# Retention by tiles with a carried state, and row transposes in two halves, in a one-core decoder layer

## The chip, the core and the metric

The kernel runs on one core of a Trainium2 chip. The metric is the device time of one execution in microseconds. A core has TensorE (matmuls; PE in the profile, its weight loads PEld), VectorE (DVE), ScalarE (ACT), GpSimd (POOL) and SyncE (SP), which here only issues DMAs. Each engine takes its own instructions in order and waits on semaphores for the others. TensorE writes to PSUM, eight banks of 128 partitions by 512 fp32 values.

## What is computed

The reference is one decoder layer on 512 tokens of width 1024. Cut to what the change touches:

```python
def _retention(q, k, v):            # 8 heads of 64, chunks of c = 128
    log_g = log(1 - 2 ** (-5 - arange(h)))
    dmat = where(diff >= 0, exp(log_g * diff), 0)
    scores = einsum('bhnid,bhnjd->bhnij', qc, kc) * dmat
    inner = einsum('bhnij,bhnjd->bhnid', scores, vc)
    kv = einsum('bhnjd,bhnje->bhnde', kc * k_dec, vc)
    # state' = g_chunk * state + kv; cross = (qc @ state) * q_dec
    return inner + cross

def _moe(xt, ...):                  # 32 experts, top 4
    hgu = xb @ w_up_gate[e] + b_up_gate[e]
    hact = x_glu * sigmoid(1.702 * x_glu) * (x_lin + 1)
    return hact @ w_down[e] + b_down[e]
```

Ahead of these stand a norm, one input projection and stick-breaking attention, whose result is yA; the retention's result, normed by groups and gated, is yB. Both go through one output projection with a residual. Behind the experts come a gate and a small projection of a per-layer input.

## The kernel before

The kernel is written in a tile framework. Outside of blocks with an order by hand, a planner puts each engine's instructions in order at build time, by the order in the program, by readiness and by its own cost estimates. On the chip that order is fixed.

**Projections and attention.** `proj` multiplies x by slices of the input weights, split into a high and a low part (`split`, L158, L159), three matmuls for each product. `ret_qk` (L326) takes the retention's q and k: `evacuate` gives four row tiles `ns` of 128 tokens, each normed and rotated on VectorE (L338 to L341); q is multiplied by its norm (L343), and k's norm is kept in `rkr` for later. `to_T` transposes them into `rqT` and `rkT`, with two heads side by side on the 128 partitions. `val` makes `vR`, whose mean over each head is taken off at L580 to L582.

**Retention, L593 to L632.** A loop over four pairs of heads (`hp`). For each tile `b` of 128 keys, the scores of that tile against all queries from it on (L607: 512, 384, 256 and 128 columns) go to PSUM banks 0 to 3 in rotation (`zbank`); VectorE scales them by the key's norm and by a decay table made by ScalarE (L613 and L599; the table has a zero above the diagonal through `dif`, L422 to L426), and L618 multiplies them by `vR` into `py`, bank 4 or 5. The two heads of a pair use two halves of the TensorE array. Behind the tiles stands a chain: copy and square on ScalarE, a mean over the head by a matmul (L625), Ln and Exp, two VectorE operations, and the split into the two parts of yB (L631, L632).

**Output projection.** `wo_half` (L635) adds for one row tile and half of the columns twelve 512-column matmuls in bank 6 or 7 and one VectorE add into `acc`. The yA half of it stands behind the retention in the program, without an order by hand: 96 matmuls. The yB half, the router and what follows are in an order by hand from L862 on. The tiles of the early pools are freed behind the retention; SyncE's next loads (L672 on) wait for that.

**Expert loop.** The 32 experts' weights, 12 MB each, pass through a ring of nine slots of 2 MB; six pieces an expert, four for `up` and two for `down`. SyncE issues the next piece into a slot when TensorE has read the old one (`load_behind`). For each expert: `up` (L1103), `act_in` and `act_out` on VectorE and ScalarE (L1139 to L1147), `up32` (L1117) if more than 64 rows were routed to it, `turn_in` for the next expert's rows, `h_T` (L1153) and `down` (L1161) in three steps, `dispatch`, which gathers the rows of the expert after the next, and `down32` (L1174). `turn_in` transposes the 96 gathered rows of the next expert, eight transposes in two banks and two ScalarE copies (`turn`, L914 to L920). `turn`, `h_T`, `spread` and `down32` take their banks from `dbank`, which alternates between 2 and 3.

Of the kernel before, what the change touches and what calls it, by code (L numbers as in the profile page):

```python
# [8 lines left out]
F32 = mybir.dt.float32  # L9
# [4 lines left out]
AF = mybir.ActivationFunctionType  # L14
ALU = mybir.AluOpType
# [4 lines left out]
P = 128  # L20
S = 512
NT = S // P
D = 1024
KD = D // P
HD = 64
NH = 8
NP = NH // 2
E = 32
# [11 lines left out]
C = 96  # L40
# [10 lines left out]
def layer_kernel(ctx, tc, a, out, dbg=None, stop=None):  # L51
    nc = tc.nc
# [48 lines left out]
    def bank(i, name):  # L101
        return ps.tile([P, 512], F32, name=name, tag=f"b{i}")
# [223 lines left out]
    def ret_qk(w, name, key, tag, ahead=0):  # L326
        ns = evacuate(proj(w, name, ahead), name)
        dst = early.tile([P, NP, S], F32, name=name + "T", tag=tag)
        rst = early.tile([P, NT, NH], F32, name=name + "r")
        for t in range(NT):  # L330
            n = ns[t]
            r, _ = headnorm_rstd(n, f"{name}{t}", rst[:, t, :])
            m = e2.tile([P, 512], F32, name=f"m{name}{t}", tag="tmp")
            nv, mv = heads(n), heads(m)
            for h in range(2):
                o = slice(h * 32, h * 32 + 32)
                s2 = slice(32 - h * 32, 64 - h * 32)
                nc.vector.tensor_tensor(mv[:, :, o], nv[:, :, s2],  # L338
                                        stab[key][:, t, None, o].to_broadcast([P, NH, 32]), op=ALU.mult)
            nc.vector.tensor_tensor(nv, nv, ctab[key][:, t, None, :].to_broadcast([P, NH, HD]), op=ALU.mult)  # L340
            nc.vector.tensor_tensor(n, n, m, op=ALU.add)  # L341
            if key == "q":
                nc.vector.tensor_tensor(nv, nv, r[:, :, None].to_broadcast([P, NH, HD]), op=ALU.mult)  # L343
            to_T(n, dst, t, None, f"{name}{t}")
        return dst, rst

    def val(w, name, ahead=0):
        banks = proj(w, name, ahead)
# [70 lines left out]
    nc.gpsimd.memset(gmean, 0.0)  # L419
    for h in range(2):  # L420
        nc.gpsimd.memset(gmean[h * HD:(h + 1) * HD, h * HD:(h + 1) * HD], 1.0 / HD)
    dif = early.tile([P, S], F32, name="dif")  # L422
    nc.gpsimd.iota(dif, pattern=[[1, S]], base=0, channel_multiplier=-1, allow_small_or_imprecise_dtypes=True)
    msk = e2.tile([P, S], F32, name="msk", tag="tmp")
    nc.vector.tensor_scalar(msk, dif, 0.0, 1.0e6, op0=ALU.is_lt, op1=ALU.mult)
    nc.vector.tensor_tensor(dif, dif, msk, op=ALU.add)  # L426


    yA, yB = [mid.tile([P, 2, NP, S], F32R, name=f"y{i}", tag=f"y{i}") for i in "AB"]
# [2 lines left out]
    def zbank(name, ids):  # L432
        zn[0] += 1
        return bank(ids[zn[0] % len(ids)], name)
# [117 lines left out]
            last_silu = nc.scalar.activation(gD[:, c, :], gD[:, c, :], AF.Silu)  # L552
    with tc.issue_after(last_silu.ins):
        nc.scalar.preload_act_table_set("natural_log_exp_and_others")
    rkT, rkr = ret_qk(w_rk, "rk", "k", "kT", 200)
    wo, woh, wol = [], [], []

    def by_rows(t):
# [31 lines left out]
    wo_split(1, fresh(1, "woh1", F32R), fresh(2, "wol1", F32R))  # L590
    load(0)

    for hp in range(NP):  # L593
        hss = [slice(j * HD, (j + 1) * HD) for j in range(2)]
        decs = []
        for j in range(2):
            h = 2 * hp + j
            dec = e2.tile([P, S], F32, name=f"dec{h}", tag="tmp")
            nc.scalar.activation(dec, dif, AF.Exp, scale=math.log(1.0 - 2.0 ** (-5.0 - h)))  # L599
            decs.append(dec)  # L600
        py = bank(4 + hp % 2, f"ry{hp}")
        for b in range(NT):
            N = S - b * P
            zs, scs = [], []
            for j in range(2):
                z = zbank(f"rz{hp}{j}{b}", (0, 1, 2, 3))
                nc.tensor.matmul(z[:, :N], rkT[hss[j], hp, b * P:(b + 1) * P], rqT[hss[j], hp, b * P:S],  # L607
                                 start=True, stop=True)
                zs.append(z)
            for j in range(2):  # L610
                h = 2 * hp + j
                sc = e2.tile([P, N], F32, name=f"rs{h}{b}", tag=f"wt{b}")
                nc.vector.scalar_tensor_tensor(sc, zs[j][:, :N], rkr[:, b, h:h + 1], decs[j][:, :N],  # L613
                                               op0=ALU.mult, op1=ALU.mult)
                scs.append(sc)
            for j in range(2):
                h = 2 * hp + j
                nc.tensor.matmul(py[hss[j], b * P:S], vR[:, b, h * HD:(h + 1) * HD], scs[j],  # L618
                                 start=b == 0, stop=b == NT - 1)
        yc = e2.tile([P, S], F32, name=f"yc{hp}", tag="tmpn", bufs=4)  # L620
        nc.scalar.copy(yc, py)
        sq = e2.tile([P, S], F32, name=f"rsq{hp}", tag="tmpn", bufs=4)
        nc.scalar.activation(sq, yc, AF.Square)
        var = zbank(f"var{hp}", (0, 1, 2, 3))
        nc.tensor.matmul(var, gmean, sq, start=True, stop=True)  # L625
        nc.scalar.activation(sq, var, AF.Ln, bias=eps)
        nc.scalar.activation(sq, sq, AF.Exp, scale=-0.5)
        nc.vector.scalar_tensor_tensor(yc, yc, pcol[:, GN_G + hp:GN_G + hp + 1], sq, op0=ALU.mult, op1=ALU.mult)
        nc.vector.scalar_tensor_tensor(yc, yc, pcol[:, GN_B + hp:GN_B + hp + 1], gD[:, hp, :],
                                       op0=ALU.add, op1=ALU.mult)  # L630
        nc.scalar.activation(yB[:, 0, hp, :], yc, AF.Copy)  # L631
        nc.vector.tensor_tensor(yB[:, 1, hp, :], yc, f32(yB[:, 0, hp, :]), op=ALU.subtract)  # L632
# [253 lines left out]

    def dbank(name):
        dn[0] += 1
        return bank(2 + dn[0] % 2, name)

    def spread(e, name):
        rk = dbank("rk" + name)
# [18 lines left out]
        xgs[e] = xg_tile(f"{e}")  # L911
        return gather(rk, C, slot, xgs[e], f"{e}")

    def turn(xg, n, xT, name):  # L914
        for h in range(2):
            pt = dbank(f"px{name}{h}")
            pv = pt[:, 0:4 * n].rearrange("p (k s) -> p k s", s=n)
            for k in range(4):
                nc.tensor.transpose(pv[:, k, :], xg[0:n, (4 * h + k) * P:(4 * h + k + 1) * P], ident[0:n, 0:n])  # L919
            nc.scalar.copy(xT[:, 4 * h:4 * h + 4, 0:n], pv)  # L920
# [157 lines left out]

    xTs = {}

    def turn_in(e):
        xTs[e] = ringC.tile([P, KD, C], F32, name=f"xT{e}", tag="xT")
        turn(xgs[e], C, xTs[e], f"{e}")

    def two(j):
        return slice(j * 64, (j + 1) * 64)
# [198 lines left out]
    for e in range(E):  # L1285
# [211 lines left out]
```

## Time and profile before

| what | us |
|---|---|
| median of 3 runs (1484.51 to 1488.26) | 1484.77 |
| the profiled execution | 1485.39 |
| its span, first to last instruction | 1483.5 |
| TensorE busy in it | 1353.6 (91%) |
| VectorE, ScalarE, GpSimd busy | 451.4, 293.3, 182.4 |

Durations come from the profiled execution. The mean granted TensorE clock is 0.985 of full speed. A record of a matmul overlaps the next one's, since matmuls are pipelined: the time that one takes in a stream is read from start to start. fp32 matmuls appear as two instructions each, so that a pair of heads makes four. A DMA share is the busy share of the core's 16 DMA engines; records that touch make it go to 1.01 or 1.02. An idle time in brackets names what the engine waited for; PEq and DVEq are the engine's own instruction stream.

### The profile page before, as it was taken

What the parts mean: (1) busy time and instruction counts of PE and PEld (TensorE: products, weight loads), DVE (VectorE), ACT (ScalarE), POOL (GpSimd) and SP (SyncE); (2) the same over time, 40 slices, a digit from 0 to 9 for tenths busy, and PEclk for the clock granted to TensorE, in tenths of its full rate; (3) what the DMA queues carried; (4) which work ended last, traced back from release to release, by engine and by line L of the source; (5) the groups of instructions that cost most, each with busy time, mean ns of one, the idle gap of its engine ahead of it and who ended that gap; (6) DMA issues with size and microseconds to landing.
All of it is one profiled execution on the core that took longest, in us unless ns stands there. A gap on an engine that the chain in (4) does not pass through costs nothing. (4 is left out here: it accounts for less than half of the span.)

```text
span 1483.5 us, 21634 instructions
## 1 busy us (share of the span) xinstructions
PE 1353.6 (91%) x8629; PEld 652.0 (44%) x8629; DVE 451.4 (30%) x1033; ACT 293.3 (20%) x564; POOL 182.4 (12%) x268
## 2 busy tenths in 40 slices
PE   8999999997999999999988899878999889799788
PEld 6776775463333334334333333323333333233256
DVE  4657497545111111111211111111111121032353
ACT  5645674341010000000000001000000000111133
POOL 3132000011110111010101011000111100212230
PEclk9999999998999999999999999999999999999999
DMA  7202504167999999999999999999999999989931
GB/s 286 85 29 79 143 25 170 38 250 278 362 375 410 408 390 403 413 411 414 412 392 411 410 408 412 411 397 417 408 410 394 374 413 408 398 346 403 420 131 57
DMA packets 65528, 474.81 MB, mean 320 GB/s; under 512 B 9485, under 2 KB 10033, under 8 KB 32401
## 3 DMA queue, kind: packets, MB, share of 16 engines
q1 hardware_dynamic: 54192, 441.69, 74.7%
q0 software_dynamic: 11200, 31.22, 6.0%
q8 instruction: 97, 1.59, 0.4%
q14 instruction: 39, 0.31, 0.1%
HBM read 454.40 MB, written 18.48 MB: 319 GB/s over the span
## 5 line engine op out<-in xcount | busy, mean ns | idle before, releaser
L1161 PE MATMUL yb<-ring,hT 128*64 128x512 f32 x1024 | 245.6, 612 | 35.3 <-DVE hT L1154 27.4
L1103 PE MATMUL glu<-ring,xT 128*64 128x512 f32 x1024 | 247.6, 599 | 16.3 <-DMA ring<-in_w_up_gate_dram 16.3
L1103 PE MATMUL lin<-ring,xT 128*64 128x512 f32 x1024 | 245.5, 594 | 0.0
L1139 DVE TENSOR_SCALAR gl<-glu 128x512 f32<-128x512 f32 x32 | 22.1, 692 | 530.7 <-PE glu L1103 530.7
L1103 PEld LDWEIGHTS glu<-ring,xT 128*64 128x64 f32 x1024 | 81.9, 138 | 145.5 <-issue 115.8
L1103 PEld LDWEIGHTS lin<-ring,xT 128*64 128x64 f32 x1024 | 83.0, 137 | 139.5 <-issue 139.5
L1161 PEld LDWEIGHTS yb<-ring,hT 128*64 128x64 f32 x1024 | 65.7, 137 | 152.8 <-issue 100.8
L903 POOL DMA_INDIRECT xg<-hn_d,idx x32 | 30.5, 954 | 781.3 <-DVE idx L902 469.0
L1117 PE MATMUL u<-ring,xT 128*32 128x256 f32 x2048 | 113.3, 379 | 0.0
L1140 ACT ACTIVATE sg<-gl 128x512 f32<-128x512 f32 x32 | 20.1, 629 | 408.8 <-DVE gl L1139 408.8
L1117 PEld LDWEIGHTS u<-ring,xT 128*32 128x32 f32 x2048 | 61.6, 110 | 47.4
L1174 PE MATMUL yc<-ring,hv 128*32 128x256 f32 x1024 | 58.6, 381 | 8.3 <-DVE hv L1170 8.3
L1185 ACT COPY y<-yb 128x512 f32<-128x512 f32 x31 | 18.1, 585 | 231.9 <-PE yb L1161 222.1
L920 ACT COPY xT<-px 128x384 f32<-128x384 f32 x64 | 27.7, 482 | 155.5 <-PE px L919 155.4
L1174 PEld LDWEIGHTS yc<-ring,hv 128*32 128x32 f32 x1024 | 31.6, 110 | 31.3 <-DVE hv L1170 12.1
L919 PE MATMUL px<-ident,xg 96*128 96x96 f32 x256 | 28.9, 258 | 15.4 <-PEq L1314 8.1
L1187 POOL DMA_DIRECT2D y_d<-y x62 | 33.7, 548 | 68.7 <-ACTq L1334 39.1
L919 PEld LDWEIGHTS px<-ident,xg 96*128 96x128 f32 x256 | 23.2, 145 | 34.9 <-issue 24.2
L1181 POOL DMA_DIRECT2D y_d<-yv x64 | 31.6, 501 | 54.5 <-ACT yv L1179 48.4
L1403 PE MATMUL o<-gh,z 128*128 128x512 f32 x128 | 37.3, 400 | 0.2 <-ACT z L1360 0.2
L899 DVE SCALAR_TENSOR_TENSOR scr<-rk,slot,iot 96x512 bf16<-96x512 f32 x32 | 23.9, 746 | 40.9 <-PE rk L893 40.9
L1141 DVE TENSOR_TENSOR gl<-gl,sg 128x512 f32<-128x512 f32 x32 | 22.2, 692 | 24.4 <-ACT sg L1140 23.7
(960 smaller groups left out, 1694.5 us busy)
## 6 DMA issues: line engine op xcount, KB each, us to landing
ring<-in_w_up_gate_dram SPq DMA_DIRECT2D x127, 2048.0 KB, 23.6
ring<-in_w_down_dram SPq DMA_DIRECT2D x128, 1024.0 KB, 23.0
ring<-in_w_in_dram SPq DMA_DIRECT2D x12, 1024.0 KB, 5.3
y_d<-y POOLq DMA_DIRECT2D x62, 128.0 KB, 9.7
ring<-in_w_out_dram SPq DMA_DIRECT2D x4, 1024.0 KB, 6.7
ring<-in_w_ple_gate_dram SPq DMA_DIRECT2D x2, 2048.0 KB, 22.0
y_d<-none SPq DMA_DIRECT2D x2, 1984.0 KB, 12.0
ring<-in_x_dram SPq DMA_DIRECT2D x4, 512.0 KB, 5.4
```

Of the source, the lines that this page charges most:

```text
L899: nc.vector.scalar_tensor_tensor(scr[0:n], rk[0:n], slots[0:n], iot[0:n], op0=ALU.is_equal, op1=ALU.mult, accum_out=idf[0:n])
L903: nc.gpsimd.indirect_dma_start(out=xg[0:n], out_offset=None, in_=hn_d, in_offset=bass.IndirectOffsetOnAxis(ap=idx[0:n, :1], axis=0))
L919: nc.tensor.transpose(pv[:, k, :], xg[0:n, (4 * h + k) * P:(4 * h + k + 1) * P], ident[0:n, 0:n])
L920: nc.scalar.copy(xT[:, 4 * h:4 * h + 4, 0:n], pv)
L1103: nc.tensor.matmul(o[two(j)], xTs[e][:, 2 * m + c, 0:64], w[:, c, f:f + 512], start=False, stop=m == 3 and c == 1)
L1117: nc.tensor.matmul(u32[four(q), g * 256:(g + 1) * 256], xTs[e][:, 2 * m + c, 64:C], w[:, c, f:f + 256], start=False, stop=m == 3 and c == ...
L1141: nc.vector.tensor_tensor(gl, gl, sg, op=ALU.mult)
L1161: nc.tensor.matmul(y64[two(j)], hT[:, fc, :], w[:, fc % 4, j * 512:(j + 1) * 512], start=fc == 0, stop=fc == KD - 1)
L1174: nc.tensor.matmul(y32[four(q), 0:256], hT[:, fc % 2, fc // 2, :], w[:, fc % 4, q * 256:(q + 1) * 256], start=fc == 0, stop=fc == KD - 1, ...
L1181: nc.gpsimd.dma_start(y_d[e * C + 64:(e + 1) * C, q * 256:(q + 1) * 256], y[four(q)])
L1187: nc.gpsimd.dma_start(y_d[e * C:e * C + 64, j * 512:(j + 1) * 512], y[two(j)])
L1403: nc.tensor.matmul(banks[t, h], (zh, zl, zh)[i][:, k, ts], (g_h, g_h, g_l)[i][k // 4][:, k % 4, hs], start=first, stop=last)
```

## The change

The retention no longer computes the scores of a key tile against all later queries. The decay is split into a factor of the query's place and one of the key's place in its tile of 128; both go into the norm factors of q and k (`decay`), so that k is multiplied by its norm as well, and one mask `causal` of 128x128 does for all scores of a tile against itself. What earlier tiles add comes from a state of 64 by 64 per head: 24 matmuls `rkn` by `vR` in banks 6 and 7, and five VectorE operations that add and decay the states of three tiles. For each pair of heads there are then eight 128-column scores, two masks of 128x512, six matmuls of state by q and eight by `vR`. The `dif` table, its mask and the eight exponentials of it go.

In the expert loop, `turn_in` is split: the first half of the next expert's rows is transposed ahead of the first `h_T`, the second half ahead of the second `h_T`, and the first four `down` steps follow in one go. `dbank` rotates through banks 2, 3 and 4.

```diff
     def ret_qk(w, name, key, tag, ahead=0):
...
-        rst = early.tile([P, NT, NH], F32, name=name + "r")
         for t in range(NT):
             n = ns[t]
-            r, _ = headnorm_rstd(n, f"{name}{t}", rst[:, t, :])
+            r, _ = headnorm_rstd(n, f"{name}{t}")
+            nc.vector.tensor_tensor(r, r, decay[key], op=ALU.mult)
...
-            if key == "q":
-                nc.vector.tensor_tensor(nv, nv, r[:, :, None].to_broadcast([P, NH, HD]), op=ALU.mult)
+            nc.vector.tensor_tensor(nv, nv, r[:, :, None].to_broadcast([P, NH, HD]), op=ALU.mult)
             to_T(n, dst, t, None, f"{name}{t}")
-        return dst, rst
+        return dst, ns
...
-    dif = early.tile([P, S], F32, name="dif")
-    nc.gpsimd.iota(dif, pattern=[[1, S]], base=0, channel_multiplier=-1, allow_small_or_imprecise_dtypes=True)
-    msk = e2.tile([P, S], F32, name="msk", tag="tmp")
-    nc.vector.tensor_scalar(msk, dif, 0.0, 1.0e6, op0=ALU.is_lt, op1=ALU.mult)
-    nc.vector.tensor_tensor(dif, dif, msk, op=ALU.add)
+    lng = [math.log(1.0 - 2.0 ** (-5.0 - h)) for h in range(NH)]
...
+    for key, sign in (("q", 1.0), ("k", -1.0)):
+        decay[key] = early.tile([P, NH], F32, name="decay" + key)
+        for h in range(NH):
+            nc.gpsimd.memset(decay[key][:, h:h + 1], sign * lng[h])
+        nc.scalar.activation(decay[key], decay[key], AF.Exp, scale=place_col)
+    tile_decay = early.tile([P, NP], F32, name="tile_decay")
...
+    causal = early.tile([P, P], F32, name="causal")
+    nc.vector.tensor_scalar(causal, jp, 0.0, None, op0=ALU.is_ge)
...
-    rkT, rkr = ret_qk(w_rk, "rk", "k", "kT", 200)
+    rkT, rkn = ret_qk(w_rk, "rk", "k", "kT", 200)
...
+    kvb = [bank(6 + i, f"kv{i}") for i in range(2)]
+    states = []
+    for b in range(NT - 1):
+        kv = kvb[b // 2][:, b % 2 * 256:b % 2 * 256 + 256]
+        for h in range(NH):
+            nc.tensor.matmul(kv[hss[h % 2], h // 2 * HD:h // 2 * HD + HD], rkn[b][:, h * HD:(h + 1) * HD],
+                             vR[:, b, h * HD:(h + 1) * HD], start=True, stop=True)
+        st = e2.tile([P, 256], F32, name=f"st{b}", tag=("wt1", "wt1", "wt2")[b])
...
+        if b == 0:
+            nc.vector.tensor_tensor(sv, kv.rearrange("p (c d) -> p c d", d=HD), fall, op=ALU.mult)
+        else:
+            nc.vector.tensor_tensor(st, states[-1], kv, op=ALU.add)
+            nc.vector.tensor_tensor(sv, sv, fall, op=ALU.mult)
+        states.append(st)
+
     for hp in range(NP):
...
-            dec = e2.tile([P, S], F32, name=f"dec{h}", tag="tmp")
-            nc.scalar.activation(dec, dif, AF.Exp, scale=math.log(1.0 - 2.0 ** (-5.0 - h)))
-            decs.append(dec)
-        py = bank(4 + hp % 2, f"ry{hp}")
+            zs.append(zbank(f"rz{hp}{j}", (0, 1, 2, 3)))
         for b in range(NT):
-            N = S - b * P
-            zs, scs = [], []
+            ts = slice(b * P, (b + 1) * P)
             for j in range(2):
-                z = zbank(f"rz{hp}{j}{b}", (0, 1, 2, 3))
-                nc.tensor.matmul(z[:, :N], rkT[hss[j], hp, b * P:(b + 1) * P], rqT[hss[j], hp, b * P:S],
-                                 start=True, stop=True)
-                zs.append(z)
+                nc.tensor.matmul(zs[j][:, ts], rkT[hss[j], hp, ts], rqT[hss[j], hp, ts], start=True, stop=True)
+        for j in range(2):
+            sc = e2.tile([P, S], F32, name=f"rs{2 * hp + j}", tag="wt0")
+            nc.vector.tensor_tensor(sc.rearrange("p (b t) -> p b t", t=P), zs[j].rearrange("p (b t) -> p b t", t=P),
+                                    causal[:, None, :].to_broadcast([P, NT, P]), op=ALU.mult)
+            scs.append(sc)
+        for b in range(1, NT):
+            ts = slice(b * P, (b + 1) * P)
+            for j in range(2):
+                nc.tensor.matmul(py[hss[j], ts], states[b - 1][hss[j], hp * HD:(hp + 1) * HD], rqT[hss[j], hp, ts],
+                                 start=b == 1, stop=False)
+        for b in range(NT):
+            ts = slice(b * P, (b + 1) * P)
             for j in range(2):
                 h = 2 * hp + j
-                sc = e2.tile([P, N], F32, name=f"rs{h}{b}", tag=f"wt{b}")
-                nc.vector.scalar_tensor_tensor(sc, zs[j][:, :N], rkr[:, b, h:h + 1], decs[j][:, :N],
-                                               op0=ALU.mult, op1=ALU.mult)
-                scs.append(sc)
-            for j in range(2):
-                h = 2 * hp + j
-                nc.tensor.matmul(py[hss[j], b * P:S], vR[:, b, h * HD:(h + 1) * HD], scs[j],
-                                 start=b == 0, stop=b == NT - 1)
+                nc.tensor.matmul(py[hss[j], ts], vR[:, b, h * HD:(h + 1) * HD], scs[j][:, ts], start=False,
+                                 stop=b == NT - 1)
...
-        return bank(2 + dn[0] % 2, name)
+        return bank(2 + dn[0] % 3, name)
...
-    def turn(xg, n, xT, name):
-        for h in range(2):
+    def turn(xg, n, xT, name, halves=range(2)):
+        for h in halves:
...
-    def turn_in(e):
-        xTs[e] = ringC.tile([P, KD, C], F32, name=f"xT{e}", tag="xT")
-        turn(xgs[e], C, xTs[e], f"{e}")
+    def turn_in(e, h):
+        if e < E:
+            if h == 0:
+                xTs[e] = ringC.tile([P, KD, C], F32, name=f"xT{e}", tag="xT")
+            turn(xgs[e], C, xTs[e], f"{e}", (h,))
...
-        if e + 1 < E:
-            turn_in(e + 1)
+
+        turn_in(e + 1, 0)
         h_T(h, hT, 0, f"{e}a")
-        down(e, hT, (0, 1))
+        turn_in(e + 1, 1)
         h_T(h, hT, 1, f"{e}b")
-        down(e, hT, (2, 3))
+        down(e, hT, (0, 1, 2, 3))
```

## Rows read from the trace of the kernel before

**Rows 1.** Window: stretch, length, busy us PE, PEld, DVE, ACT, POOL; clock, DMA share, GB/s.

```profile
236.08:299.18 63.10, 61.36 (x233) 30.01 (x233) 40.02 (x85) 21.97 (x33) 2.16 (x5) 1.00 0.39 137
```

**Rows 2.** Windows in the expert loop, from the first expert to the 29th.

```profile
349.40:390.30 40.90, 37.81 (x318) 14.82 (x319) 16.32 (x74) 2.75 (x6) 2.06 (x3) 0.98 0.89 350
390.30:453.30 63.00, 58.94 (x430) 21.99 (x427) 11.17 (x27) 5.22 (x11) 6.93 (x12) 1.00 0.93 366
453.30:1113.00 659.70, 605.98 (x4438) 240.36 (x4437) 113.92 (x275) 49.90 (x102) 61.54 (x102) 0.99 1.01 407
1113.00:1180.50 67.50, 61.74 (x430) 22.81 (x427) 11.26 (x27) 5.31 (x11) 6.94 (x12) 0.95 0.96 388
...
1279.60:1313.60 34.00, 31.27 (x131) 11.13 (x131) 7.55 (x14) 4.48 (x10) 4.76 (x5) 0.95 0.87 350
```

**Rows 3.** Groups by shape: busy us, mean ns; idle before. TensorE, retention stage.

```profile
L163 PE MATMUL pjo<-woh,yA 128*128 128x512 f32 x32 | 13.2, 412 | 0.0
...
L625 PE MATMUL var<-rsq,gmean 128*128 128x512 f32 x8 | 4.4, 634 | 0.3 <-ACT rsq L623 0.3
```

**Rows 4.** Timeline (start, us, engine, line) of TensorE: yA matmuls, first of yB.

```profile
298.25 0.40 PE L165 MATMUL pjo<-woh,yA 128*128 128x512 f32 x1
...
299.18 0.40 PE L163 MATMUL pjo<-woh,yB 128*128 128x512 f32 x1
```

**Rows 5.** Timeline of TensorE: pairs of heads, in the attention and in the retention.

```profile
102.75 2.86 PE L512 MATMUL py<-wt,vS 128*64 128x512 f32 x16 [0.60 <-ACT wt L504]
105.54 0.70 PE L469 MATMUL z<-sqT,skT 64*128 64x256 f32 x4
...
236.08 1.92 PE L607 MATMUL rz<-rqT,rkT 64*128 64x512 f32 x8
237.93 0.50 PE L163 MATMUL pjo<-woh,yA 128*128 128x512 f32 x1
...
259.10 0.49 PE L607 MATMUL rz<-rqT,rkT 64*128 64x128 f32 x4
259.52 0.50 PE L163 MATMUL pjo<-woh,yA 128*128 128x512 f32 x1
...
269.55 0.49 PE L607 MATMUL rz<-rqT,rkT 64*128 64x128 f32 x2
```

**Rows 6.** Timeline of VectorE: the mean of vR, its first and last operation.

```profile
234.81 1.39 DVE L580 TENSOR_REDUCE vm<-vR 128x8 f32<-128x512 f32 x2 [2.71 <-ACT vR L351]
...
240.77 0.68 DVE L582 TENSOR_TENSOR vR<-vR,vm 128x512 f32<-128x512 f32 x1
```

**Rows 7.** Groups by shape on VectorE: 128x256 and 128x512 operations.

```profile
L338 DVE TENSOR_TENSOR mrk<-nrk,stk 128x256 f32<-128x256 f32 x8 | 3.1, 418 | 0.0
...
L340 DVE TENSOR_TENSOR nrk<-nrk,ctk 128x512 f32<-128x512 f32 x4 | 2.7, 687 | 0.1
```

**Rows 8.** Timelines of VectorE and SyncE: the last yB, the next ring loads.

```profile
292.07 0.69 DVE L632 TENSOR_TENSOR yB<-yc,yB 128x512 fp32r<-128x512 f32 x1
...
293.71 6.49 SPq L224 DMA_DIRECT2D ring<-in_w_up_gate_dram  x3
```

**Rows 9.** Timeline of TensorE: an expert with more than 64 rows.

```profile
700.79 0.88 PE L919 MATMUL px<-ident,xg 96*128 96x96 f32 x8
...
707.61 0.49 PE L893 MATMUL rk<-rankT,ident_r 32*128 32x512 f32 x1
...
708.03 3.65 PE L1161 MATMUL yb<-ring,hT 128*64 128x512 f32 x16
```

**Rows 10.** Timeline of TensorE and VectorE: an expert with up to 64 rows.

```profile
730.83 0.85 PE L919 MATMUL px<-ident,xg 96*128 96x96 f32 x8 [0.31 <-PEq L1314]
...
731.36 0.42 DVE L1147 SCALAR_TENSOR_TENSOR h<-h,gl 128x256 f32<-128x256 f32 x1
...
737.66 0.50 PE L893 MATMUL rk<-rankT,ident_r 32*128 32x512 f32 x1
```

**Rows 11.** Timeline of TensorE: its first matmul of the 29th expert.

```profile
1279.65 0.67 PE L1097 MATMUL glu<-bst,bsel 96*64 96x512 bf16 x2 [7.17 <-PEq L992]
```

More of the change, by code (lines that the diff above doesn't have):

```diff
@@ L421, in layer_kernel @@
         nc.gpsimd.memset(gmean[h * HD:(h + 1) * HD, h * HD:(h + 1) * HD], 1.0 / HD)
-    dif = early.tile([P, S], F32, name="dif")
-    nc.gpsimd.iota(dif, pattern=[[1, S]], base=0, channel_multiplier=-1, allow_small_or_imprecise_dtypes=True)
-    msk = e2.tile([P, S], F32, name="msk", tag="tmp")
-    nc.vector.tensor_scalar(msk, dif, 0.0, 1.0e6, op0=ALU.is_lt, op1=ALU.mult)
-    nc.vector.tensor_tensor(dif, dif, msk, op=ALU.add)
+    lng = [math.log(1.0 - 2.0 ** (-5.0 - h)) for h in range(NH)]
+    place_col = early.tile([P, 1], F32, name="place_col")
+    nc.gpsimd.iota(place_col, pattern=[[0, 1]], base=0, channel_multiplier=1, allow_small_or_imprecise_dtypes=True)
+    decay = {}
+    for key, sign in (("q", 1.0), ("k", -1.0)):
[5 more added lines that the diff above has]
+    for h in range(NH):
+        nc.gpsimd.memset(tile_decay[h % 2 * HD:h % 2 * HD + HD, h // 2:h // 2 + 1], math.exp(P * lng[h]))
+    causal = early.tile([P, P], F32, name="causal")
+    nc.vector.tensor_scalar(causal, jp, 0.0, None, op0=ALU.is_ge)
     yA, yB = [mid.tile([P, 2, NP, S], F32R, name=f"y{i}", tag=f"y{i}") for i in "AB"]
@@ L591, in layer_kernel @@
     load(0)
+    hss = [slice(j * HD, (j + 1) * HD) for j in range(2)]
+    kvb = [bank(6 + i, f"kv{i}") for i in range(2)]
+    states = []
+    for b in range(NT - 1):
+        kv = kvb[b // 2][:, b % 2 * 256:b % 2 * 256 + 256]
+        for h in range(NH):
+            nc.tensor.matmul(kv[hss[h % 2], h // 2 * HD:h // 2 * HD + HD], rkn[b][:, h * HD:(h + 1) * HD],
+                             vR[:, b, h * HD:(h + 1) * HD], start=True, stop=True)
+        st = e2.tile([P, 256], F32, name=f"st{b}", tag=("wt1", "wt1", "wt2")[b])
+        sv = st.rearrange("p (c d) -> p c d", d=HD)
+        fall = tile_decay[:, :, None].to_broadcast([P, NP, HD])
+        if b == 0:
[4 more added lines that the diff above has]
+        states.append(st)
@@ L593, in layer_kernel @@
     for hp in range(NP):
-        hss = [slice(j * HD, (j + 1) * HD) for j in range(2)]
-        decs = []
+        py = bank(4 + hp % 2, f"ry{hp}")
+        zs, scs = [], []
         for j in range(2):
-            h = 2 * hp + j
-            dec = e2.tile([P, S], F32, name=f"dec{h}", tag="tmp")
-            nc.scalar.activation(dec, dif, AF.Exp, scale=math.log(1.0 - 2.0 ** (-5.0 - h)))
-            decs.append(dec)
-        py = bank(4 + hp % 2, f"ry{hp}")
+            zs.append(zbank(f"rz{hp}{j}", (0, 1, 2, 3)))
@@ L610, in layer_kernel @@
+        for b in range(NT):
+            ts = slice(b * P, (b + 1) * P)
             for j in range(2):
                 h = 2 * hp + j
-                sc = e2.tile([P, N], F32, name=f"rs{h}{b}", tag=f"wt{b}")
-                nc.vector.scalar_tensor_tensor(sc, zs[j][:, :N], rkr[:, b, h:h + 1], decs[j][:, :N],
-                                               op0=ALU.mult, op1=ALU.mult)
-                scs.append(sc)
-            for j in range(2):
-                h = 2 * hp + j
-                nc.tensor.matmul(py[hss[j], b * P:S], vR[:, b, h * HD:(h + 1) * HD], scs[j],
-                                 start=b == 0, stop=b == NT - 1)
+                nc.tensor.matmul(py[hss[j], ts], vR[:, b, h * HD:(h + 1) * HD], scs[j][:, ts], start=False,
+                                 stop=b == NT - 1)
```

## The prediction

> **What bounds the kernel now.** I read the stretches one by one, because what ends last differs from stage to stage. In the retention stage, from the end of the v projection to the first output-projection matmul on yB, TensorE is busy for 61.36 of 63.10 us at full clock, while VectorE has 40.02 and the DMA engines 0.39 [rows 1]. The reader is to see there that TensorE bounds this stage, and that no gap of VectorE or ScalarE does: where a retention matmul isn't ready, the planner puts one of the yA output projection in its place. In the expert loop two resources are full at once. From the fourth expert to the 23rd the DMA engines are at 1.01 with 407 GB/s, and TensorE at 606 of 660 us [rows 2]. A share of 1.01 is what I call full. In four shorter stretches the share is below it: 0.89, 0.93, 0.96 and 0.87, which makes 40.9 x 0.12 + 63 x 0.08 + 67.5 x 0.05 + 34 x 0.14 = 4.9 + 5.0 + 3.4 + 4.8 = 18.1 us in which the DMA engines had nothing to do, because TensorE had not freed a slot of the ring [rows 2]. So TensorE time saved in the expert loop is worth at most what it fills of these 18 us, and time saved ahead of the loop is worth its full amount, because the whole stream of loads starts earlier by it.
>
> **The retention stage.** TensorE's 61.4 us hold 96 yA matmuls (three groups of 32, of which one stands in [rows 3]) at a pitch of 0.93 / 4 = 0.233 us [rows 4], that is 22.4 us. The variance matmuls are 4.4 us [rows 3]. Neither changes. The rest, 61.4 - 22.4 - 4.4 = 34.6 us, is the score and output matmuls: per pair of heads 2 x (512 + 384 + 256 + 128) = 2560 columns for the two heads side by side, 10240 over the four pairs. That is 3.4 ns per column of a pair. The pair works on two halves of the array, and what it costs when the two run together is seen twice: 896 columns (512 and 384) in 237.93 - 236.08 = 1.85 us, 2.1 ns each, and in the attention stage 1280 columns in 105.54 - 102.75 = 2.79 us, 2.2 ns each [rows 5]. A lone pair of 128 columns takes 259.52 - 259.10 = 0.42 us, about 0.15 more than 128 x 2.1, and the record of a single 128-column matmul, without its partner, is as long as the pair's, 0.49 us with the overlap [rows 5].
>
> The change has per pair of heads four score pairs, three state pairs and four output pairs, all of 128 columns: 1408 columns, 5632 over four. It adds 24 matmuls of 64 columns for the states, 12 pairs and 768 columns. Together 6400 pair columns. At 2.2 ns that is 14.1 us. The kinds change 3 times per pair of heads and once for each of 3 blocks of the state, 15 times 0.15 = 2.3 us. Sum 16.4 us. The bounds: if every pair stood alone at 0.42 us, (44 + 12) x 0.42 = 23.5 us; if every matmul stood alone, (88 + 24) x 0.42 = 47 us, which would be more than the 34.6 of now. I take 16.4, because the new code issues eight scores, six state products and eight outputs one after the other with all inputs there, as the attention stage does with its eight outputs, and that is the row with 2.2 ns. Saved: 34.6 - 16.4 = 18.2 us, with bounds 11.1 (pairs alone) and 20.5 (no cost of change).
>
> The lone pair's 0.15 us has a rule behind it that speaks against the change. The Trainium skill, "TensorEngine Tiling (Array Packing)", section Key Properties, says that changing the tiling mode, not just the tile, drains TensorE. The change brings a third mode into each pair of heads (64 rows by 64 columns for the state products, beside 64 by 128 and 128 by 64). The trace agrees with a cost per change of this order; without it the new sum would be 14.1 instead of 16.4 us.
>
> What stands against the gain is the start. vR must have its mean taken off before the first state matmul, and VectorE ends that at 240.77 + 0.68 = 241.45, while the projection ends at 236.08 [rows 5, 6]. Banks 6 and 7, where the state blocks lie, are the banks of the yA matmuls, so that filler is shut out until VectorE has read the last state block. The scores of two pairs of heads can run meanwhile (their four banks are free), 8 x 0.42 = 3.4 us at the dear price, and the first two state blocks follow as their vR tiles come. The stall is between 0 and 5.4 us; I take 2, since 3.4 us of it is covered. Five 128x256 operations of 0.42 us [rows 7] for the states come on VectorE there, 2.1 us, ahead of eight masks of 128x512, 0.69 us each [rows 7]; in exchange the 32 scalings of the scores go and eight exponentials leave ScalarE. VectorE had 23 us to spare [rows 1], so this costs nothing while filler is there, and up to the 5.4 us already in the bound if not.
>
> Ahead of the stage, the k tiles get one more 128x512 multiply each, 4 x 0.69 = 2.7 us of VectorE [rows 7], in the v projection, where TensorE is again the bound. The splits that feed it come first in VectorE's order, and VectorE still waits 2.7 us at that stretch's end [rows 6], so I take zero, with 0 to 2.7 for the range. The decay tables, some 24 small fills on GpSimd and two small exponentials, take the place of a 128x512 iota and two VectorE operations, all behind the first projections; zero, since TensorE waits for none of them there.
>
> Net for the stage: 18.2 - 2 = 16 us, bounds 11.1 - 5.4 - 2.7 = 3 and 20.5. The last yB is at 292.07 + 0.69 = 292.8 [rows 8], 6.4 us ahead of the stage's end at 299.18 [rows 4], and everything behind is in an order written by hand. SyncE's loads of the ring issue at 293.71, as soon as the early tiles are free [rows 8]; they come earlier too and land ahead of the loop.
>
> **The expert loop.** Now the two halves of the row transposes run together; h_T waits for ScalarE's copy of the first half, because both use bank 2 or 3, then each down pair waits for VectorE's copy of its hT. In an expert with more than 64 rows this takes from 700.79 to the next kind of matmul at 707.61, 6.8 us [rows 9]. In the new order the second half of the transposes covers the first copy, and the second h_T the rest: four groups of 0.44 (the eight transposes take 0.88 together [rows 9]), then 16 down matmuls of 0.22 us (the sixteen from 708.03 take 3.65 with the tail of the last [rows 9]), 1.8 + 3.5 = 5.3 us, 1.5 saved. In an expert with up to 64 rows the h of the first half is there only at 731.36 + 0.42 = 731.8 [rows 10], so the first half of the transposes is followed by a wait of 0.5 us, and 0.9 is saved of the 6.8 us from 730.83 to 737.66 [rows 10]. A third bank in the rotation costs nothing; bank 4 has no reader in the loop. That is 1.5 us for about half the experts and 0.9 for the others, some 37 us of TensorE, but the DMA engines allow only what fills their 18.1 us. The 4.9 of the first expert lie ahead of the first reordered transposes: none. Of the next 5.0, the advance of two experts: 2.9. Of 3.4 behind four full experts in a row: all. Of the 4.8 at the 29th, where TensorE waited 7.2 us at a branch that the change doesn't touch [rows 11]: 1. Sum 7 us; bounds 0 and 5.0 + 3.4 + 4.8 = 13.
>
> **Sum.** The profiled execution took 1485.39 us (span 1483.5 and 1.9 around it), 0.6 above the median of 1484.77. 1485.4 - 16 - 7 = 1462 us.
>
> **Rivals.**
> *The loop gives nothing back.* The DMA engines at 1.01 through most of the loop speak for it [rows 2]: every shorter expert then only waits longer for its weights. 1485.4 - 16 = 1469 us.
> *Pairs at the price of a lone pair.* 23.5 instead of 16.4 us: 1485.4 - 11.1 + 2 - 7 = 1469 us. For it: the planner now puts yA matmuls between pairs [rows 5]. Against: these fill waits for VectorE, of which the new order has fewer. The Trainium skill, "TensorE: Matmul & The Clock Gate", section Back-to-back issue gap, gives 81 ns as the sustained spacing at 128 columns where a matmul by itself takes 56; by that ratio 14.1 us would be about 20, an estimate, and the time about 1466. No row here isolates it.
> *The chain decides, and the change doesn't shorten the stage as it should.* If the last yB comes no earlier, only the 6.4 us of filler behind it [rows 4, 8] can be lost: 1485.4 - 6.4 - 7 = 1472 us. Against it: VectorE's spare time [rows 1], and a chain that has one step of scores per pair of heads in place of four.
> *Slower.* Each matmul runs without its partner. Its place is the retention stage, its price 112 x 0.42 = 47 us against 34.6, so 1485.4 + 12.4 + 2 - 7 = 1493 us. It decides from a mean slot of (34.6 - 2 + 7) / 112 = 0.35 us on. For it: single score matmuls stand in the trace, as at 269.55, and cost as much as a pair [rows 5]. Against it: they are single because the two heads' scalings end 0.7 us apart, while the new products of both heads are ready together.
> *Better than forecast.* Both parts near their upper ends, 1485.4 - 20.5 - 13 = 1452 us.
>
> **How the numbers follow.** Forecast (1456 to 1468) 50%, no gain in the loop 18%, pairs alone 14%, chain 8%, slower 5%, better 5%. The range reaches from the best case to somewhat beyond the chain's, 1450 to 1475; left out are the slower case and the tails of the others. A measurement of this kernel can tell about 0.3% from no change, 4.5 us: all cases but the slower one lie beyond it, with small tails of "chain" and of a poor start within it: faster 0.90, same 0.05, slower 0.05.
>
> **What would show it.** The stage from the end of the v projection to the first yB matmul should be 47 us, at full clock, with TensorE idle for 2 to 4 us, nearly all in the first 7 us. The retention matmuls should stand in groups, eight 128-column ones in about 1 us. In the loop the DMA share should be full in the stretches that had 0.93 and 0.96, px and ph should alternate with no idle before the second down group, and TensorE's waits for ring loads should grow. It would be wrong if the granted clock falls in the stage's first microseconds, if matmuls of the two heads do not start together, or if the loop's length, 964 us for the first 29 experts now, from the first window's start to the last one's end [rows 2], stays as it is.

## The result and the profile after

The changed kernel takes 1462.4 us (median of 4 runs, 1460.6 to 1462.9) against 1486.0 for the kernel before on the same chip: a ratio of 0.984, 95% interval 0.982 to 0.986. The forecast was 1462, in a range from 1450 to 1475. The profiled execution has a span of 1458.8 us, 24.7 less than before. Three places hold that: up to the loop's start 17.5 us (17.6 at the end of the retention stage), in the expert loop 6.1, in the tail behind it 1.1.

The first windows of the changed kernel: stretch, length, busy us of TensorE (PE), weight loads, VectorE, ScalarE, GpSimd, granted clock, DMA share, GB/s. The first row is the retention stage, the others stretches of the expert loop; they answer to [rows 1, 2].

```profile
236.58:281.62 45.04, 44.37 (x330) 32.80 (x329) 32.84 (x67) 18.10 (x27) 2.08 (x5) 1.00 0.60 211
...
331.90:370.80 38.90, 38.31 (x316) 15.17 (x315) 16.36 (x74) 2.85 (x6) 2.06 (x3) 0.95 0.88 344
370.80:431.10 60.30, 58.26 (x428) 22.29 (x425) 11.17 (x27) 5.34 (x11) 6.96 (x12) 1.00 0.98 390
431.10:1085.70 654.60, 605.51 (x4440) 241.54 (x4439) 114.03 (x275) 51.97 (x102) 61.65 (x102) 0.99 1.01 409
1085.70:1146.10 60.40, 58.34 (x429) 22.91 (x425) 11.17 (x27) 5.38 (x11) 6.96 (x12) 1.00 1.01 407
...
1252.60:1285.00 32.40, 30.93 (x129) 11.82 (x129) 7.48 (x14) 4.49 (x10) 4.78 (x5) 0.93 0.92 370
...
1352.40:1399.50 47.10, 30.68 (x114) 9.64 (x113) 18.70 (x20) 7.94 (x10) 14.15 (x9) 0.86 0.89 370
```

The stage went from 63.1 to 45.04 us and is still TensorE's, at full clock, with 0.67 us idle. In the loop the share of the DMA engines is now full in the stretch that had 0.96 and nearly so where it had 0.93; the long stretch in the middle is as full as before, and TensorE's busy time in it didn't change. The last row is the last expert: 47.1 us, where the kernel before needed 39.5 (the same columns):

```profile
1383.60:1423.10 39.50, 27.50 (x114) 8.46 (x113) 15.33 (x19) 7.99 (x10) 10.21 (x8) 1.00 0.96 397
```

The stage's beginning on TensorE, from the last matmul of the v projection (start, length, line, operation; x counts instructions, two for each fp32 matmul), the last operation of VectorE on yB, and the first yB matmul [rows 4, 5, 8]:

```profile
236.26 0.39 PE L165 MATMUL pjvR<-wsvR7h,xl 128*128 128x512 f32 x1
236.58 0.86 PE L629 MATMUL rz<-rqT,rkT 64*128 64x128 f32 x8
237.65 0.69 PE L609 MATMUL kv<-vR,nrk 128*64 128x64 f32 x16 [0.20 <-DVE vR L591]
238.26 1.60 PE L629 MATMUL rz<-rqT,rkT 64*128 64x128 f32 x16
239.79 1.33 PE L609 MATMUL kv<-vR,nrk 128*64 128x64 f32 x32
241.06 0.44 PE L638 MATMUL ry<-rqT,st 64*64 64x128 f32 x4
241.42 1.16 PE L629 MATMUL rz<-rqT,rkT 64*128 64x128 f32 x8
242.51 0.43 PE L638 MATMUL ry<-rqT,st 64*64 64x128 f32 x4
...
247.48 1.09 PE L644 MATMUL ry<-rs,vR 128*64 128x128 f32 x16
248.51 0.44 PE L638 MATMUL ry<-rqT,st 64*64 64x128 f32 x4
...
268.88 0.69 DVE L658 TENSOR_TENSOR yB<-yc,yB 128x512 fp32r<-128x512 f32 x1
...
281.62 0.40 PE L163 MATMUL pjo<-woh,yB 128*128 128x512 f32 x1
```

The reader is to see three things. There is next to no gap: scores of both first pairs of heads stand between the state blocks. Eight output matmuls of 128 columns, 16 instructions, take from 247.48 to 248.51, 1.03 us, as they would in four pairs; but the 8 instructions from 241.42 to 242.51, four scores of one head, take 1.09 as well. And the last yB is done at 269.6, 12 us ahead of the stage's end.

In the loop, one expert with more than 64 rows and one with up to 64, in the new order [rows 9, 10]:

```profile
672.30 0.55 PE L945 MATMUL px<-ident,xg 96*128 96x96 f32 x4
672.69 0.38 PE L1181 MATMUL ph10a<-ident,h 128*128 128x128 f32 x2
672.91 0.49 PE L945 MATMUL px<-ident,xg 96*128 96x96 f32 x4
673.48 0.44 PE L1181 MATMUL ph10b<-ident,h 128*128 128x128 f32 x2
673.85 3.65 PE L1189 MATMUL yb<-ring,hT 128*64 128x512 f32 x16
677.43 0.50 PE L919 MATMUL rk<-rankT,ident_r 32*128 32x512 f32 x1
...
1342.49 0.52 PE L945 MATMUL px<-ident,xg 96*128 96x96 f32 x4 [0.31 <-PEq L1342]
1343.59 0.41 PE L1181 MATMUL ph30a<-ident,h 128*128 128x128 f32 x2 [0.58 <-DVE h L1174]
1343.84 0.49 PE L945 MATMUL px<-ident,xg 96*128 96x96 f32 x4
1344.39 0.41 PE L1181 MATMUL ph30b<-ident,h 128*128 128x128 f32 x2
1344.73 7.09 PE L1189 MATMUL yb<-ring,hT 128*64 128x512 f32 x32
```

From the first px to rk it is 677.43 - 672.30 = 5.1 us in place of 6.8. From expert to expert, where TensorE doesn't wait for a load, it is 35.2 us instead of 36.9, and 25.1 instead of 26.1 with up to 64 rows. What became of that shows in TensorE's waits in the loop (engine, line, releaser: us in total, times, longest), first of the kernel before:

```profile
PE yb L1161 <- DVE hT L1154: 27.4, 49, 1.9
PE glu L1103 <- DMA ring<-in_w_up_gate_dram: 16.3, 10, 2.6
```

and after:

```profile
PE glu L1131 <- DMA ring<-in_w_up_gate_dram: 45.0, 22, 8.8
...
PE yb L1189 <- DVE hT L1182: 1.2, 1, 1.2
```

The wait for hT is all but gone, and the wait for the ring's loads has grown by 28.7 us. The new order saves TensorE waits, not busy time.

### The profile page after: what moved, and what is told of

Same layout as the page of the kernel before. It is cut to its first block, busy times and chain, and to the rows that moved or that the text cites. A ratio compares the mean times of both kernels' runs of the same rounds, so it can differ in the third digit from the quotient of the medians.

```text
span 1458.8 us, 21861 instructions
## 1 busy us (share of the span) xinstructions
PE 1336.9 (92%) x8725; PEld 656.3 (45%) x8725; DVE 447.6 (31%) x1025; ACT 291.5 (20%) x558; POOL 186.3 (13%) x292
## 3 DMA queue, kind: packets, MB, share of 16 engines
q8 instruction: 97, 1.59, 0.4%
## 5 line engine op out<-in xcount | busy, mean ns | idle before, releaser
L1131 PE MATMUL glu<-ring,xT 128*64 128x512 f32 x1024 | 257.2, 621 | 45.1 <-DMA ring<-in_w_up_gate_dram 45.0
L1189 PE MATMUL yb<-ring,hT 128*64 128x512 f32 x1024 | 236.5, 605 | 1.2 <-DVE hT L1182 1.2
L1189 PEld LDWEIGHTS yb<-ring,hT 128*64 128x64 f32 x1024 | 69.4, 138 | 126.7 <-issue 122.2
L946 ACT COPY xT<-px 128x384 f32<-128x384 f32 x64 | 30.7, 480 | 164.4 <-PE px L945 163.3
L925 DVE SCALAR_TENSOR_TENSOR scr<-rk,slot,iot 96x512 bf16<-96x512 f32 x32 | 23.9, 747 | 76.7 <-PE rk L919 76.7
L945 PE MATMUL px<-ident,xg 96*128 96x96 f32 x256 | 33.6, 255 | 12.3 <-DMA xg<-hn_d,idx 5.5
L945 PEld LDWEIGHTS px<-ident,xg 96*128 96x128 f32 x256 | 25.5, 143 | 31.8 <-PEq L1342 16.4
```

The lines of the kernel that those rows point to most:

```text
L925: nc.vector.scalar_tensor_tensor(scr[0:n], rk[0:n], slots[0:n], iot[0:n], op0=ALU.is_equal, op1=ALU.mult, accum_out=idf[0:n])
L1131: nc.tensor.matmul(o[two(j)], xTs[e][:, 2 * m + c, 0:64], w[:, c, f:f + 512], start=False, stop=m == 3 and c == 1)
L1189: nc.tensor.matmul(y64[two(j)], hT[:, fc, :], w[:, fc % 4, j * 512:(j + 1) * 512], start=fc == 0, stop=fc == KD - 1)
```

## The experiments

**Each part alone.** The retention by tiles with the old order and two banks in the loop:

```
-        turn_in(e + 1, 0)
-        h_T(h, hT, 0, f"{e}a")
-        turn_in(e + 1, 1)
-        h_T(h, hT, 1, f"{e}b")
-        down(e, hT, (0, 1, 2, 3))
+        turn_in(e + 1, 0)
+        turn_in(e + 1, 1)
+        h_T(h, hT, 0, f"{e}a")
+        down(e, hT, (0, 1))
+        h_T(h, hT, 1, f"{e}b")
+        down(e, hT, (2, 3))
```

> The retention by tiles alone: the expert loop has its old order of row transposes and two banks. Theory of the two parts adding up (my account): the stage gives 17.6 us and the loop part is missing, so about 1486.0 - 17.6 = 1468 us, and the loop keeps its length of about 1074 us. Rival, the loop gains because it starts with its loads earlier or later than its matmuls: 1462 us again, the loop about 6 us shorter. Rival, the loop takes the gain back by waits for loads: 1475 us or more.

The other half, the retention as before and the new order with three banks, the same lines the other way round:

> The order of the row transposes and the third bank alone, with the retention as before. My account: the loop gives about 6 us, what fits into the stretches in which the loads had stopped, so 1480 us, and the retention stage stays at 63.1 us. Rival, the loop's part gives nothing by itself: 1486. Rival, TensorE bounds the loop and each expert gives its 1.7 or 1.0 us: 1486 - 42 = 1444.

Measured: 1467.8 us (ratio 0.9875, 0.9857 to 0.9894) and 1478.7 us (0.9955, 0.9940 to 0.9969), the kernel before at 1485.2. So 17.4 and 6.5 us; their sum, 23.9, is close to the 23.6 that the two give together. The stage is 45.09 us long in the first, as in the full change. The rivals by which the loop takes the stage's gain back, or gives nothing by itself, are out; so is the one by which TensorE alone bounds the loop, which asked for 1444 us of the second run.

**The third bank.**

```
-        return bank(2 + dn[0] % 3, name)
+        return bank(2 + dn[0] % 2, name)
```

> The changed kernel with two banks in the rotation again instead of three. What I predicted of the third bank was that it costs nothing; what it brings wasn't counted by itself. If the new order lives on the third bank (with two, the first transpose of the activated rows waits for ScalarE's copy of the first half, and the second half of the row transposes for VectorE's copy), an expert loses about 0.5 to 0.9 us of TensorE, but as the loads bound the loop, only a part of the 6 us of the loop shows: 1463 to 1468 us. If the bank does nothing: 1462.

Measured: 1461.7 us (0.984, 0.9826 to 0.9853), no difference. On its timeline of TensorE the second half of the row transposes waits for ScalarE's copy of the first:

```profile
675.90 0.38 PE L1181 MATMUL ph10a<-ident,h 128*128 128x128 f32 x2
676.69 0.55 PE L945 MATMUL px<-ident,xg 96*128 96x96 f32 x4 [0.40 <-ACT xT L946]
```

An expert takes 35.5 or 25.4 us, 0.3 more than with three banks, less than the 0.5 to 0.9 that I had expected. The loads hide all of it.

**What the new order is worth when the loads have room.** In the changed kernel, and then in the kernel before, 25 MB of the stream aren't loaded, and the matmuls read what the slots held:

```
-                for i in halves:
+                for i in (halves if not (c == 5 and 4 <= e < E - 4) else (0,)):
                     nc.sync.dma_start(v[:, i, :], src[:, i, :])
```

> The changed kernel; of the experts 4 to 27 the second half of the last quarter-down piece (1 MB of 12.6 for each expert) isn't loaded, and the matmuls use what the slot held: 25 MB less, at 409 GB/s 61 us less of the loads' time, with the same work on all engines. Theory that the loads bound the loop: it falls by most of TensorE's 45 us of waits for loads, to 1405 to 1420 us. Rival, TensorE bounds it: a few us at most, 1455 to 1462.

> The kernel before with the same 25 MB left unloaded (second half of the last down piece of the experts 4 to 27). It tells what the new order of transposes is worth when the loads have room. Theory: TensorE then bounds the loop in both kernels, the kernel before falls only by about its 16 us of waits for loads, to 1465 to 1470 us, and stands 45 to 60 us behind the changed kernel with the same loads left out (17.6 us of the stage and 1.7 or 1.0 us for each of 24 or more experts). Rival, the loads bound both anyway: it falls by 60 us as well, to about 1425, and the distance stays at 23 us.

Measured: 1407.1 us for the changed kernel (0.9475, 0.9451 to 0.9499), 1460.9 for the one before (0.9837, 0.9812 to 0.9862). The same edit is worth 55 us to the one and 25 to the other, so the changed kernel was bound by its loads and the other one only in part. The 25 are more than the 16 of waits for loads that I had expected there: in the profiled executions those waits fall by 12.2 us and TensorE's busy time by 4.6 (1353.6 to 1349.0), and I haven't traced the rest. TensorE's waits for ring loads, first in the changed kernel so cut:

```profile
PE glu L1131 <- DMA ring<-in_w_up_gate_dram: 7.2, 1, 7.2
```

and in the kernel before so cut:

```profile
PE yb L1161 <- DVE hT L1154: 27.5, 49, 1.9
...
PE glu L1103 <- DMA ring<-in_w_up_gate_dram: 4.1, 2, 2.3
```

The distance between the two is 53.8 us. Less the 17.6 of the stage, that is 36 us for the order of the transposes once the loads hardly decide. TensorE itself needs some 40 us less: from the first expert's first matmul to the last one's it is 966.9 us against 1010.6, which is 43.7 with up to 4.1 of the old order's waits for loads in them, and 7.2 go back in the one wait that is left, at the last expert. With the full stream 6 us are left.

**Matmuls without their partner.** The scores, the state products and the outputs are issued head by head; for the scores:

```
-        for b in range(NT):
-            ts = slice(b * P, (b + 1) * P)
-            for j in range(2):
+        for j in range(2):
+            for b in range(NT):
+                ts = slice(b * P, (b + 1) * P)
                 nc.tensor.matmul(zs[j][:, ts], ...)
```

> The changed kernel with the same retention matmuls, but issued head by head: four scores of one head, then four of the other, and so the state products and the outputs, so that neighbours in TensorE's order no longer work on different halves of the array. Theory that the two heads run side by side (2.2 ns per column of a pair): 44 pairs become 88 matmuls of about 0.27 us, 44 x 0.27 = 12 us more on TensorE, which bounds the stage: about 1474 us, the stage 57 us. Rival, a matmul without its partner costs the 0.42 us of the slower case of the prediction: 88 x 0.42 = 37 against 44 x 0.28 = 12.3 us, about 1487 us. Rival, the pairs didn't run side by side anyway, or the time is hidden: 1462, the stage 45 us.

Measured: 1463.5 us (0.9849, 0.9825 to 0.9874), not distinguishable from the changed kernel. The stage is 2.7 us longer; its busy time has grown by 3.4 us, and no idle time is left in it (the window of the stage, columns as above):

```profile
238.12:285.87 47.75, 47.75 (x329) 36.82 (x329) 32.93 (x67) 18.17 (x27) 2.15 (x5) 1.00 0.56 199
```

The eight outputs of a pair of heads take 250.94 - 249.43 = 1.51 us, not 1.03 (timeline of TensorE):

```profile
249.43 1.58 PE L644 MATMUL ry<-rs,vR 128*64 128x128 f32 x16
250.94 0.87 PE L638 MATMUL ry<-rqT,st 64*64 64x128 f32 x8
```

So 2.7 us where I had expected 12. Three reasons stand in the starts of the single instructions. A 128-column instruction by itself is followed by the next after 0.11 us, a matmul thus by 0.22, not 0.27; the two of a pair start within 7 ns of each other, and the next pair 0.11 us behind them. The changed kernel had less to lose: only half of its score instructions start beside a partner. And the edit didn't take the pairs apart wholly: where one head's group ends and the other's begins, the starts come every 0.05 us, which I read as instructions of both heads in turn. The run shows that a matmul without its partner costs about half of the 0.42 us that my slower rival put on it.

**What hid the start.** The scores get two banks, the variances the other two:

```
-            zs.append(zbank(f"rz{hp}{j}", (0, 1, 2, 3)))
+            zs.append(bank(j, f"rz{hp}{j}"))
...
-        var = zbank(f"var{hp}", (0, 1, 2, 3))
+        var = bank(2 + hp % 2, f"var{hp}")
```

> The changed kernel with the scores of the retention in two banks instead of four, and the variances in the other two. It asks what hid the stall that I priced at 2 us and that didn't come. Theory: the scores of the second pair of heads, which fill TensorE's first 5 us beside those of the first while VectorE takes the means off; with two banks they can't, TensorE is idle for 1 to 2 us there, and the stage is 46 to 48 us instead of 45: 1463 to 1465 us. Rival, the first scores and the state blocks suffice: the stage and the time stay, 1462.

Measured: 1465.5 us (0.9857, 0.9840 to 0.9875), the stage 47.73 us with 1.59 idle (window of the stage):

```profile
237.16:284.89 47.73, 46.14 (x330) 33.83 (x329) 33.05 (x67) 18.08 (x27) 2.16 (x5) 1.00 0.57 199
```

Its beginning on TensorE's timeline:

```profile
238.83 0.72 PE L629 MATMUL rz<-rqT,rkT 64*128 64x128 f32 x8
240.32 0.69 PE L609 MATMUL kv<-vR,nrk 128*64 128x64 f32 x16 [0.77 <-DVE st L615]
```

The scores of the second pair of heads were the cover: without them TensorE waits 0.77 us for VectorE's first state, and the order that the planner then makes is dearer by another 1.8 us of busy time; it changes the kind of matmul 35 times in the stage instead of 29.

**What the last expert gives back.** TensorE waits 8.8 us at the last expert, behind a load of 2 MB of the last gate's weights. First that load goes to the end of the stream:

```
-    items.insert(items.index((E - 1, 0)), "g0")
-    items.append("g1")
+    items += ["g0", "g1"]
```

> The changed kernel, with the first half of the last gate's weights (2 MB) loaded behind the last expert's pieces instead of ahead of them. Theory: at the end the loads bound the loop, TensorE waits 8.8 us for a piece of the last expert, and the 2 MB take about 5 us of the loads' time ahead of it; the last expert ends about 5 us earlier, and the gate's weights, needed only behind it, come late by less: about 1457 to 1459 us. Rival, the end is bound by the sum of all bytes, those of the gate included: 1462. Rival, the splits of the gate's weights now stand on the path behind the loop: 1465 us or more.

Measured: 1470.9 us (0.9905, 0.9888 to 0.9922), 8.5 us slower than the changed kernel. The last of the three held: the last down matmuls start 7 us earlier, and then TensorE waits for VectorE, whose splits of the late weights stand ahead of the last rows (timeline of TensorE):

```profile
1380.06 9.25 PE L1188 MATMUL yb<-ring,hT 128*64 128x512 f32 x32 [0.79 <-DVE hT L1181]
1406.42 1.32 PE L1227 MATMUL pc<-yl,oh 64*128 64x512 f32 x4 [17.11 <-DVEq L1457]
```

Then between the gate and the down pieces, together with the changed kernel once more for the comparison, and with two of VectorE's splits moved back:

```
-    items.insert(items.index((E - 1, 0)), "g0")
+    items.insert(items.index((E - 1, 4)), "g0")
```

> The changed kernel itself, unaltered, for a comparison with the next two on the same chip. Expected as before: about 1462 us, 0.984 of the kernel before.

> The changed kernel, with the first half of the last gate's weights loaded between the last expert's gate pieces and its down pieces, instead of ahead of all of them. With that load at the very end its splits on ScalarE and VectorE came 17 us after the last matmul of the expert. Theory: the gate pieces land 5 us earlier, TensorE's wait of 8.8 us at the last expert shrinks, the down pieces land as now, and the splits still lie beside the down matmuls: 1457 to 1460 us. Rival, VectorE's order behind the last expert (three splits, four additions) sets the end and nothing changes: 1462. Rival, the splits come late again: 1465 or more.

> As the run before it, and two of VectorE's three splits of the gate's weights (1.9 us each) move behind the sums of the first two tiles, where TensorE has 16 matmuls to do. Theory: TensorE's wait of 3.4 us ahead of the last join goes too: 1453 to 1457 us. Rival, the moved splits delay the halves that TensorE needs next: 1460 or more.

Measured: the changed kernel 1462.9 us (1461.8 to 1464.9), with the load in the middle 1458.1 (1455.9 to 1459.2; ratio to the kernel before 0.9807, 0.9792 to 0.9822), with the splits moved too 1457.5 (0.9804, 0.9788 to 0.9820). The load's place is worth 4.8 us, and the runs of the two don't overlap; this version beats both kernels. Moving the splits adds nothing that shows (1453 to 1457 us were expected): TensorE now waits for the last down pieces, 3.6 us in all with the load in the middle and 5.3 with the splits moved too. In the former:

```profile
1388.12 1.94 PE L1189 MATMUL yb<-ring,hT 128*64 128x512 f32 x8 [1.51 <-DMA ring<-in_w_down_dram]
1391.89 1.94 PE L1189 MATMUL yb<-ring,hT 128*64 128x512 f32 x8 [1.84 <-DMA ring<-in_w_down_dram]
1395.45 0.83 PE L1228 MATMUL pc<-yl,oh 64*128 64x512 f32 x4 [1.62 <-DVEq L1458]
```

## Why the prediction was right, step by step

**What bounds the kernel.** Right in both places. TensorE time ahead of the loop counted in full (17.4 us alone), and of the 36 us that the loop's new order gives when the loads have room 6 counted; the two cut streams show that the loads are the reason.

**The retention matmuls.** I summed 16.4 us for the new ones. The stage's 44.37 us of TensorE, less 22.4 of yA and 4.3 of variances, leave 17.7. The sum is close, its terms are not. The pair's price was too high: among their like a pair of 128-column instructions comes every 0.11 us, 2 x 0.11 / 128 = 1.7 ns per column of a pair, where I took 2.2 from stretches that hold changes of kind as well [rows 5]; that makes 10.9 us of my 14.1. Against that, the planner issued a part of the scores four to one head, at 0.22 us each without a partner, and it changes kind 29 times in the stage, not 15. By the starts of the 128-column instructions, the last of one kind and the first of the next are 0.20 us apart instead of 0.11, and the second of the new kind comes 0.16 us (outputs, state products) or 0.21 us (scores) behind the first. A change thus costs from 0.14 us (the lone pair of state products, 241.42 - 241.06 - 0.22) to 0.20 (the lone pair of scores, 0.42 - 0.22 [rows 5]). The 0.15 that I took was near; the count was not, and 29 changes make 4 to 6 us where I had 2.3. The rule of the Trainium skill that I weighed ("TensorEngine Tiling (Array Packing)", Key Properties: a change of the tiling mode drains TensorE) agrees with these 0.14 to 0.20 us.

**The lone pair's 0.42 us.** This was the step misread. I took its length for its price, and the equal length of a record without partner as proof that a partner is free [rows 5]. The 0.42 are 0.22 of two instructions, and the rest is the way into the kind and out of it. So two rivals stood on a wrong price: "pairs at the price of a lone pair" (23.5 us for the matmuls) and "slower" (112 x 0.42 = 47 us). At the 0.22 us of a matmul alone, 112 of them and the 4 to 6 us of changes make some 30 us at most, below the 34.6 of the kernel before; that mechanism couldn't have ended on the slower side. The ratio of the Trainium skill's "TensorE: Matmul & The Clock Gate", Back-to-back issue gap, by which I estimated the pairs at 20 us, isn't borne out here either: four pairs take 1.03 us. With the 2.3 us of changes beside them that estimate would have meant 1468 us, not the 1466 that I wrote.

**The start.** I took 2 us of stall out of 0 to 5.4; it was 0.20 us, because the scores of two pairs of heads and the state blocks interleave without a gap. The banks run shows the cover, as the text had named it, and the text should have let it count in full. The v projection ends 0.5 us later than before (236.58 against 236.08). It lies between 236.58 and 238.12 in the ten profiled executions with the new retention, and between 234.95 and 236.08 in the three with the old one, so something ahead of the stage does cost about a microsecond, and I had taken all of it as zero. The k multiplies, which I priced at zero, up to 2.7, aren't it: from its first matmul to its end the v projection takes 24.45 us, before 24.56. The delay is there already in the attention, whose first output matmuls start at 103.86 instead of 102.75 [rows 5] (timeline of TensorE), and not before 103.86 in any of the ten:

```profile
103.86 2.86 PE L521 MATMUL py<-wt,vS 128*64 128x512 f32 x16 [0.57 <-ACT wt L513]
```

What delays them stays open.

**The chain.** The last yB at 269.6, 12 us ahead of the end, against 6.4 us before: VectorE and ScalarE's chain did not decide.

**Net for the stage.** 18.1 us off its length, 17.6 of its end; 16 were forecast. Of its terms the matmuls cost 1.3 us more, and the idle time came to 0.67 us, where the forecast had the 1.7 of before and 2 of stall. That 1462 met the median of 1462.4 is in part luck: in the profiled execution, at 1460.6 the fastest of the four, the stage gave 1.6 us more than the sum had, the tail behind the loop 1.1 for which it had no term, and the loop 0.9 less.

**The loop.** An expert saves 1.7 or 1.0 us of TensorE (forecast 1.5 and 0.9). Of the idle time of the loads, taken from the shares as before [rows 2]: first expert nothing (as forecast); second and third 5.0 to 60.3 x 0.03 = 1.8, so 3.2 (2.9, for which the prediction shows no working); 24th and 25th all 3.4 (3.4); 29th 4.8 to 32.4 x 0.09 = 2.9, so 1.9 (1). That is 8.5 where I had 7, and the loop is 6.1 us shorter; shares with two digits can't tell more closely. The landing of a load can. In both kernels TensorE waits for the last expert's first piece, in the changed one until 1361.83, in the kernel before until 1386.82 (timeline of TensorE):

```profile
1386.82 1.94 PE L1103 MATMUL glu<-ring,xT 128*64 128x512 f32 x8 [2.57 <-DMA ring<-in_w_up_gate_dram]
```

That is 25.0 us earlier, 17.5 of them there at the loop's start, so the loads had gained 7.5 us in the loop up to there. From this piece to the loop's end the changed kernel takes 1.4 us more, which leaves 6.1. The last expert is what I hadn't looked at: TensorE reached it 13.7 us earlier in the loop than before, stood 8.8 us for its first piece, behind the gate's weights, where the kernel before stood 2.6 there and 2.0 at the second, and gave 7.6 back; the moved load shows that 4.8 of them could be had.

**The rest of what I said would show.** Idle of 2 to 4 us at the stage's start: not there. Eight 128-column matmuls in about 1 us: 1.03 for outputs, 1.09 for four scores of a single head. The first 29 experts: 331.9 to 1285.0, 953.1 us, against 964.2, so 11.1 us less there; the next two bring it to 13.7, and the last one takes 7.6 back.

## What to carry to other kernels

Price a small matmul among its like, start to start, and put what a group of it costs at its edges on the change of kind, counted in the order that the planner makes; a lone record's length says neither. Before counting time saved in a loop, ask whether its loads run through without pause: here 36 us became 6, and the way to know was to leave out a part of the stream in both kernels. When a loop gets nearer to its loads, look at its last turn, where what was loaded early for later use now stands in the way.

## What the runs showed of the hardware

A matmul of the other half of the array needn't be next in line to run beside its partner: issued behind all eight instructions of one head's outputs, the other head's first one started 5 ns behind the fifth of them, with three still to come, and from there the starts come every 0.05 us (run with the matmuls issued head by head). A wait on TensorE can cost more than itself. Behind the 8.8 us at the last expert eight instructions took 3.68 us, where the like of them take 1.94 later in that expert (timeline of TensorE, changed kernel), and 1.94 in the kernel before behind its 2.57 us:

```profile
1361.83 3.68 PE L1131 MATMUL glu<-ring,xT 128*64 128x512 f32 x8 [8.82 <-DMA ring<-in_w_up_gate_dram]
...
1374.87 1.94 PE L1131 MATMUL glu<-ring,xT 128*64 128x512 f32 x8
```

The granted clock of the 10 us behind the wait was 0.77, so in part at the lower of its two levels, 1.2 GHz (window of the same kernel):

```profile
1362.00:1372.00 10.00, 10.00 (x34) 3.05 (x35) 0.00 (x0) 0.00 (x0) 6.71 (x5) 0.77 1.00 423
```
